# A hybrid mixer layer on one Trainium2 core: the depthwise convolutions read a copy of their product in SBUF, and the ring of divided weight tiles has four places

## The chip, the cores and the metric

One core of a Trainium2 chip runs the whole layer in one program. The metric is the device time of one execution in microseconds; three runs of the kernel before gave a median of 1195.45 us (1193.54 to 1199.78).

## What is computed

512 tokens of width 1024, in float32. One normalised input feeds four mixers side by side, each 512 wide (RWKV-7, gated linear attention, mLSTM, SSD), whose outputs are projected, weighted by gates and added; an output product and a gated feed-forward part with a short convolution follow. The piece that the change touches is the causal depthwise convolution with four taps, followed by SiLU, ahead of the SSD (1024 channels) and of the mLSTM's queries and keys (512 channels):

```python
def causal_dwconv(x, w, b):
    k, c = w.shape
    y = lax.conv_general_dilated(x, w[:, None, :].astype(x.dtype), window_strides=(1,),
                                 padding=((k - 1, 0),), dimension_numbers=('NWC', 'WIO', 'NWC'),
                                 feature_group_count=c)
    return y + b

q, k = _split(jax.nn.silu(causal_dwconv(qk, conv_w, conv_b)), (MLSTM_DQK, MLSTM_DQK))
x, bm, cm = _split(jax.nn.silu(causal_dwconv(xbc, conv_w, conv_b)), ...)
```

## The kernel before

**Products.** A float32 weight tile of 128x512 is loaded by SyncE's queue into `raw`, ScalarE casts it to `hi` (L225), and VectorE, in some places GpSimd, subtracts to get the rest, `lo` (L226). `split_h` does this. The pairs of hi and lo come from `w_tiles` (L217), a ring with three places for each. A product is three matmuls per 128 rows of the depth, hi by hi, hi by lo and lo by hi (`mm3`, L235 to L237). With 1024 inputs a tile of 128 output channels by 512 tokens takes 24 of them and fills one PSUM bank of `psd`, which has three. `fm` makes such a tile with channels as partitions; `tm` (L330 to L332, 256 columns) makes products with tokens as partitions, two banks at a time, each bank for two blocks of 128 tokens and half of the outputs; every weight pair is used by both banks.

**Convolution.** `conv4` is called for each `fm` tile: eight for the SSD (`ssd_x`, sx0 to sx7) and four for the mLSTM (`mlstm_proj`, mq0 to mq3). ScalarE writes `y` from the bank with the last tap's weight and the bias (L904), VectorE adds the three shifted taps, reading the bank each time (L907), ScalarE takes tanh (L909), and VectorE the last product (L910). The bank is free after the third L907.

**Order.** Nothing is issued in the order of the source alone: `TileContext(schedule_with_timeline_sim=True)` (L1331) orders the instructions of all engines ahead of the run, from priorities and its own estimate of durations. At run time each engine takes its queue strictly in that order and waits for semaphores. The program's stages overlap. In time: norm, RWKV projections, first RWKV half (`rwkv_half(0)`: an inverse by 31 rounds of L600 and L602 on VectorE, 129 to 172 us, then a loop over chunks, then a group norm that ends in the matmuls of L728 at 315 us), gated linear attention (`gla`, whose U recurrence is L832, whose masks are L845 and whose products with the masks are L854) and `ssd_x` between them, the SSD (`ssd`, L995), a projection for its z gate (`ssd_z`, `tm("sz", ...)`), the second RWKV half with its own inverse (488 to 528 us), the mLSTM, the output product, and the feed-forward part from 837 us to the end.

**The SSD's chain.** For each of four blocks of 128 tokens a broadcast (`sab`, two buffers, L1019) is loaded through DRAM, GpSimd and VectorE subtract from it (L1041, four instructions each), ScalarE takes exp (L1042), GpSimd masks it (L1043), VectorE multiplies (L1052), and TensorE uses it (L1056), which frees the buffer. L1031 transposes x, L1033 copies it, L1038 and L1039 scale it, L1062 and L1068 are the state's products, L1063, L1064, L1073 and L1074 what is done with them. The z gate's banks are read by ScalarE (L1084) and VectorE (L1085).

**The feed-forward part's first two products** (`fm_halves` at L1239) need four pairs at a time; three come from the ring, the fourth is a pair of its own, `wx`, in a pool `hw`.

Of the kernel before, what the change touches and what calls it, by code (L numbers as in the profile page):

```python
# [16 lines left out]
P = 128  # L17
T = 512
# [142 lines left out]
def kernel(ctx: ExitStack, tc: tile.TileContext, A, out):  # L161
    nc = tc.nc
    V, S, G, PE = nc.vector, nc.scalar, nc.gpsimd, nc.tensor
# [23 lines left out]
    wp = ctx.enter_context(tc.tile_pool(name="wp", bufs=1))  # L187
# [7 lines left out]
    def pd():  # L195
        return dense[0].tile([P, T], F32, tag="d", name="psd")
# [17 lines left out]
    def col(name, i=0, lo=0, hi=P):  # L214
        return pf[lo:hi, PF_AT[name] + i:PF_AT[name] + i + 1]

    def w_tiles():  # L217
        return (wp.tile([P, 512], F32R, tag="hi", name="hi", bufs=3), wp.tile([P, 512], F32R, tag="lo", name="lo", bufs=3))

    def split_h(src, h, tiles=None, eng=V):  # L220
        raw = wp.tile([P, 512], F32, tag="raw", name="raw", bufs=NRAW)
# [9 lines left out]
    def split_w(src, tiles=(None, None), eng=V):  # L231
        return [split_h(src, h, tiles[h], G if (pl[0] >> h) & 1 else eng) for h in range(2)]

    def mm3(ps, lh, ll, rh, rl, first, last):
        PE.matmul(ps, lh, rh, start=first, stop=False)  # L235
        PE.matmul(ps, lh, rl, start=False, stop=False)  # L236
        PE.matmul(ps, ll, rh, start=False, stop=last)  # L237
# [36 lines left out]
    def fm_halves(jobs, eng=V):  # L274
        ws = [split_w(src, tiles, eng) for src, tiles in jobs]
        pss = [pd() for _ in jobs]
        for h in range(2):
            ts = slice(256 * h, 256 * h + 256)
            for w, ps in zip(ws, pss):
                for k in range(KD):  # L280
                    hi, lo = w[k // 4]
                    ks = slice((k % 4) * P, (k % 4 + 1) * P)
                    mm3(ps[:, ts], hi[:, ks], lo[:, ks], uh[:, k, ts], ul[:, k, ts], k == 0, k == KD - 1)
        return pss
# [53 lines left out]
    def t2(pool=None):  # L338
        pl, n = pool or wpool
        return pl.tile([P, T], F32, tag="w", name="w", bufs=n)  # L340
# [559 lines left out]
        return res  # L900

    def conv4(ps, w, b, n, i, pool=None):
        y = t2(pool)
        S.activation(y, ps, AF.Identity, scale=col(w, 3 * n + i), bias=col(b, i))  # L904
        for k in range(3):
            d = 3 - k
            V.scalar_tensor_tensor(y[:, d:T], ps[:, 0:T - d], col(w, k * n + i), y[:, d:T], op0=ALU.mult, op1=ALU.add)  # L907
        th = t2(pool)
        S.activation(th, y, AF.Tanh, scale=0.5)  # L909
        V.scalar_tensor_tensor(y, th, 1.0, y, op0=ALU.add, op1=ALU.mult)  # L910
        return y
# [80 lines left out]
    def ssd_x():  # L992
        return [conv4(fm(f"sx{i}"), "scw", "scb", 8, i, (wk, NW)) for i in range(8)]
# [215 lines left out]
    nc.sync.dma_start(gb2, A["gvec"][D:2 * D].partition_broadcast(P))  # L1209
    gb3 = hp.tile([P, D], F32, name="gb3")  # L1210
    nc.sync.dma_start(gb3, A["gvec"][2 * D:3 * D].partition_broadcast(P))
    hw_ctx = ExitStack()
    hw = hw_ctx.enter_context(tc.tile_pool(name="hw", bufs=1, side="right", reuse_waits="tile"))
    wx = [hw.tile([P, 512], F32R, name=n) for n in ("wxh", "wxl")]
    hx = ExitStack()
    np_ = hx.enter_context(tc.tile_pool(name="nq", bufs=1, side="right", reuse_waits="tile"))

# [5 lines left out]
    for b in range(NB):  # L1223
# [12 lines left out]
        norm_T(h2[:, b], gb2, b, np_, uh, ul, 1, [pr_, pm])  # L1236
    tap("h2", h2)
    hx.close()
    first = fm_halves([(A["up"][0], (None, None)), (A["up"][1], (None, (wx[0], wx[1])))])  # L1239
    hw_ctx.close()  # L1240
    wo_ctx.close()
    mo_ctx.close()
    ps_ctx.close()
# [42 lines left out]
    for n in range(2):  # L1286
# [3 lines left out]
        for k in range(NF):  # L1290
            late = n == 1 and k >= NF - KT
            tiles = tuple(fp.tile([P, 512], F32R, tag="y", name="wl", bufs=6) for _ in range(2)) if late else None
            w = split_h(A["dn"][n * (NF // 2) + k // 2], k % 2, tiles)
# [41 lines left out]
```

## Time and profile before

| | |
|---|---|
| median of three runs | 1195.45 us (1193.54 to 1199.78) |
| the profiled execution | 1195.54 us |
| its span, first to last instruction | 1193.7 us |
| TensorE, VectorE, ScalarE, GpSimd busy | 96%, 55%, 37%, 28% of the span |
| chain that ended last | 74% TensorE, 11% VectorE, 7% DMA, 4% issue |
| costliest groups | 912 matmuls each at L235, L236 and L237, 358 us a line; 280 subtracts of L226 on VectorE, 229 us |

An engine's row gives its busy time; the idle time in front of an instruction is shown with what ended it. A matmul of 512 columns shows about 0.39 us, but one starts every 0.227 us, since they overlap. PEclk is the granted TensorE clock as a share of full speed.

### The profile page before, as it was taken

The numbers are of one execution on the slowest core, as the hardware profiler recorded it, in microseconds if no ns is written. First come the engines' busy times: TensorE is split into PE (matmuls) and PEld (weight loads), VectorE is DVE, ScalarE is ACT, GpSimd is POOL, SyncE is SP. The second block draws the span as 40 slices with busy tenths as digits, with TensorE's granted clock in tenths as the row PEclk, the third lists the DMA queues.
The fourth block names the chain that finished last, engine by engine and source line by source line (L and its number), as shares of the span: only waits on it lengthen the run. The fifth ranks groups of instructions, "written<-read, shape, count | busy, mean of one in ns | idle before, by whom it ended". The sixth has DMA issues, their size and how long they took to land.

```text
span 1193.7 us, 17895 instructions
## 1 busy us (share of the span) xinstructions
PE 1143.7 (96%) x6881; PEld 928.9 (78%) x6881; DVE 651.6 (55%) x1090; ACT 444.4 (37%) x820; POOL 331.4 (28%) x287
## 2 busy tenths in 40 slices
PE   5999989999999999989999999999999999999997
PEld 4887868777788767778777777778788888888886
DVE  5258796453576365793235653554665666652323
ACT  4355234332333432232124343432444444442323
POOL 3104012230285543331114543620212222220100
PEclk9999989999998999999999999999999999999999
DMA  5222322322341322332224523561232223222322
GB/s 198 65 98 64 88 61 70 103 78 79 105 98 53 98 80 67 93 83 91 68 84 150 160 88 115 184 201 38 89 101 96 96 96 99 97 97 97 97 97 107
DMA packets 79886, 117.30 MB, mean 98 GB/s; under 512 B 22660, under 2 KB 27172, under 8 KB 79800
## 3 DMA queue, kind: packets, MB, share of 16 engines
q1 hardware_dynamic: 79224, 115.11, 30.6%
q8 instruction: 54, 0.88, 0.3%
q10 hardware_dynamic: 576, 1.05, 0.2%
q14 instruction: 32, 0.26, 0.1%
HBM read 107.93 MB, written 8.19 MB: 97 GB/s over the span
## 4 chain that ended last, share of the span: by engine, by line
PE 74%; DVE 11%; DMA 7%; issue 4%; ACT 2%; POOL 1%; SPq 1%; POOLq 0%; DVEq 0%; ACTq 0%
PE psd L235 17%; PE psd L236 16%; PE psd L237 16%; PE psd L1282 3%; PE psd L1283 3%; PE psd L1284 3%; DVE Mi L602 2%; DVE Mt L600 2%; DMA sab<-ad 2%; DVE lo L226 1%; PE psr L676 1%; PE psd L331 1%; PE psd L330 1%; DMA raw<-in_wo_dram 1%; PE psd L332 1%
## 5 line engine op out<-in xcount | busy, mean ns | idle before, releaser
L226 DVE TENSOR_TENSOR lo<-raw,hi 128x512 fp32r<-128x512 f32 x280 | 229.0, 819 | 312.0 <-ACT hi L225 300.6
L225 ACT CAST hi<-raw 128x512 fp32r<-128x512 f32 x322 | 199.6, 620 | 485.7 <-PE psd L236 300.9
L235 PE MATMUL psd<-uh,hi 128*128 128x512 f32 (+1 forms) x912 | 359.9, 395 | 11.5 <-DVE w L907 4.8
L237 PE MATMUL psd<-uh,lo 128*128 128x512 f32 (+1 forms) x912 | 357.6, 393 | 4.5 <-DVE lo L226 4.1
L236 PE MATMUL psd<-ul,hi 128*128 128x512 f32 (+1 forms) x912 | 356.2, 391 | 0.2 <-DVE ul L252 0.2
L235 PEld LDWEIGHTS psd<-uh,hi 128*128 128x128 f32 x912 | 172.2, 189 | 53.0 <-ACT hi L225 6.2
L237 PEld LDWEIGHTS psd<-uh,lo 128*128 128x128 f32 x912 | 172.2, 189 | 44.8 <-DVE lo L226 5.6
L236 PEld LDWEIGHTS psd<-ul,hi 128*128 128x128 f32 x912 | 172.3, 189 | 36.8 <-issue 2.6
L226 POOL TENSOR_TENSOR lo<-raw,hi 128x512 fp32r<-128x512 f32 x42 | 56.9, 1356 | 194.2 <-ACT hi L225 157.5
L1271 POOL TENSOR_TENSOR y<-y 128x512 f32<-128x512 f32 x22 | 28.3, 1288 | 174.0 <-DVE y L1265 160.1
L1265 DVE SCALAR_TENSOR_TENSOR y<-psd,pf,y 128x510 f32<-128x510 f32 x88 | 65.9, 750 | 2.7
L1284 PE MATMUL psd<-hi,al 128*128 128x512 f32 x164 | 63.8, 389 | 0.0
L1283 PE MATMUL psd<-lo,ah 128*128 128x512 f32 x164 | 63.8, 389 | 0.0
L331 PE MATMUL psd<-lo,uh 128*128 128x256 f32 x192 | 57.1, 298 | 1.0 <-DVE lo L226 1.0
L1282 PE MATMUL psd<-hi,ah 128*128 128x512 f32 x164 | 57.3, 389 | 0.0
L332 PE MATMUL psd<-hi,ul 128*128 128x256 f32 x192 | 56.3, 294 | 0.0
L330 PE MATMUL psd<-hi,uh 128*128 128x256 f32 x192 | 55.8, 292 | 0.0
L331 PEld LDWEIGHTS psd<-lo,uh 128*128 128x128 f32 x192 | 37.8, 197 | 5.2 <-issue 3.3
L332 PEld LDWEIGHTS psd<-hi,ul 128*128 128x128 f32 x192 | 37.9, 197 | 1.3 <-issue 1.0
L330 PEld LDWEIGHTS psd<-hi,uh 128*128 128x128 f32 x192 | 37.7, 197 | 1.6 <-issue 1.2
L1284 PEld LDWEIGHTS psd<-hi,al 128*128 128x128 f32 x164 | 30.8, 188 | 6.5
L1282 PEld LDWEIGHTS psd<-hi,ah 128*128 128x128 f32 x164 | 30.8, 188 | 6.4
(418 smaller groups left out, 1696.5 us busy)
## 6 DMA issues: line engine op xcount, KB each, us to landing
raw<-in_wfm_dram SPq DMA_DIRECT2D x140, 256.0 KB, 2.6
raw<-in_up_dram SPq DMA_DIRECT2D x88, 256.0 KB, 2.5
raw<-in_dn_dram SPq DMA_DIRECT2D x44, 256.0 KB, 2.5
raw<-in_bp_dram SPq DMA_DIRECT2D x32, 256.0 KB, 2.7
raw<-in_wtm_dram SPq DMA_DIRECT2D x24, 256.0 KB, 2.6
raw<-in_wo_dram SPq DMA_DIRECT2D x16, 256.0 KB, 3.0
gd<-th SPq DMA_DIRECT2D x15, 256.0 KB, 2.1
th<-gd SPq DMA_DIRECT2D x15, 256.0 KB, 2.9
```

The lines of the kernel that those rows point to most:

```text
L225: S.copy(hi, raw)
L226: eng.tensor_tensor(lo, raw, hi.bitcast(F32), op=ALU.subtract)
L235: PE.matmul(ps, lh, rh, start=first, stop=False)
L236: PE.matmul(ps, lh, rl, start=False, stop=False)
L237: PE.matmul(ps, ll, rh, start=False, stop=last)
L330: PE.matmul(o, uh[:, k, bs], hi[:, cs], start=first, stop=False)
L331: PE.matmul(o, uh[:, k, bs], lo[:, cs], start=False, stop=False)
L332: PE.matmul(o, ul[:, k, bs], hi[:, cs], start=False, stop=last)
L1265: V.scalar_tensor_tensor(y[:, d:T], ps[:, 0:T - d], col("fcw", k * 44 + n), y[:, d:T], op0=ALU.mult, op1=ALU.add)
L1282: PE.matmul(ps, ah[:, k, bs], hi, start=(k == 0), stop=False)
L1283: PE.matmul(ps, ah[:, k, bs], lo, start=False, stop=False)
L1284: PE.matmul(ps, al[:, k, bs], hi, start=False, stop=(k == NF - 1))
```

## The change

`conv4` takes its second tile `th` at the start, and ScalarE copies the bank into it (L904 of the new kernel). The activation (L905) and VectorE's three taps (L908) read that copy, and tanh later overwrites it. The ring of weight tiles has four places each for hi and lo. The pool `hw` with the pair `wx` is gone, and the first two products of the feed-forward part take all four pairs from the ring. From L910 on the lines of both kernels agree up to L1211; behind that the new ones are three or four lower.

```diff
--- before.py
+++ after.py
@@ -215,7 +215,7 @@
         return pf[lo:hi, PF_AT[name] + i:PF_AT[name] + i + 1]
 
     def w_tiles():
-        return (wp.tile([P, 512], F32R, tag="hi", name="hi", bufs=3), wp.tile([P, 512], F32R, tag="lo", name="lo", bufs=3))
+        return (wp.tile([P, 512], F32R, tag="hi", name="hi", bufs=4), wp.tile([P, 512], F32R, tag="lo", name="lo", bufs=4))
 
     def split_h(src, h, tiles=None, eng=V):
         raw = wp.tile([P, 512], F32, tag="raw", name="raw", bufs=NRAW)
@@ -900,12 +900,12 @@
         return res
 
     def conv4(ps, w, b, n, i, pool=None):
-        y = t2(pool)
-        S.activation(y, ps, AF.Identity, scale=col(w, 3 * n + i), bias=col(b, i))
+        y, th = t2(pool), t2(pool)
+        S.copy(th, ps)
+        S.activation(y, th, AF.Identity, scale=col(w, 3 * n + i), bias=col(b, i))
         for k in range(3):
             d = 3 - k
-            V.scalar_tensor_tensor(y[:, d:T], ps[:, 0:T - d], col(w, k * n + i), y[:, d:T], op0=ALU.mult, op1=ALU.add)
-        th = t2(pool)
+            V.scalar_tensor_tensor(y[:, d:T], th[:, 0:T - d], col(w, k * n + i), y[:, d:T], op0=ALU.mult, op1=ALU.add)
         S.activation(th, y, AF.Tanh, scale=0.5)
         V.scalar_tensor_tensor(y, th, 1.0, y, op0=ALU.add, op1=ALU.mult)
         return y
@@ -1209,9 +1209,6 @@
     nc.sync.dma_start(gb2, A["gvec"][D:2 * D].partition_broadcast(P))
     gb3 = hp.tile([P, D], F32, name="gb3")
     nc.sync.dma_start(gb3, A["gvec"][2 * D:3 * D].partition_broadcast(P))
-    hw_ctx = ExitStack()
-    hw = hw_ctx.enter_context(tc.tile_pool(name="hw", bufs=1, side="right", reuse_waits="tile"))
-    wx = [hw.tile([P, 512], F32R, name=n) for n in ("wxh", "wxl")]
     hx = ExitStack()
     np_ = hx.enter_context(tc.tile_pool(name="nq", bufs=1, side="right", reuse_waits="tile"))
 
@@ -1236,8 +1233,7 @@
         norm_T(h2[:, b], gb2, b, np_, uh, ul, 1, [pr_, pm])
     tap("h2", h2)
     hx.close()
-    first = fm_halves([(A["up"][0], (None, None)), (A["up"][1], (None, (wx[0], wx[1])))])
-    hw_ctx.close()
+    first = fm_halves([(A["up"][0], (None, None)), (A["up"][1], (None, None))])
     wo_ctx.close()
     mo_ctx.close()
     ps_ctx.close()
```

The scheduler makes a new order from this on all engines, far from the convolutions too. Three places follow. A number behind a name tells buffers apart.

**The order at the first convs.** VectorE before: steps of the first inverse (Mt, Mi), the U recurrence of the gated linear attention (L832), the conv of sx0 (bank psd_2141), and the masks L845 that read psm_1835 and psm_1836.

```order
L602 TENSOR_TENSOR Mi_845<-Mi_845,Mt_846 64x10x22
L907 SCALAR_TENSOR_TENSOR w_2166<-psd_2141,pf_77,w_2166 128x509
L600 TENSOR_TENSOR Mt_846<-Ls_842,Mi_845 64x207
L907 SCALAR_TENSOR_TENSOR w_2166<-psd_2141,pf_77,w_2166 128x510
L602 TENSOR_TENSOR Mi_845<-Mi_845,Mt_846 64x9x23
L832 SCALAR_TENSOR_TENSOR w_1779<-w_1778,gdk_1690,w_1779 128x128
L907 SCALAR_TENSOR_TENSOR w_2166<-psd_2141,pf_77,w_2166 128x511
L845 TENSOR_TENSOR w_1869<-psm_1835,cst_76 128x512
L600 TENSOR_TENSOR Mt_846<-Ls_842,Mi_845 64x192
L832 SCALAR_TENSOR_TENSOR w_1780<-w_1779,gdk_1690,w_1780 128x128
L845 TENSOR_TENSOR w_1871<-psm_1836,cst_76 128x512
```

VectorE now, the last rows ahead of the masks; in front of these stand, from the inverse step 64x10x22 on, that step and three more of the inverse, another L908, the last conv step L910 and four more L832.

```order
L602 TENSOR_TENSOR Mi_845<-Mi_845,Mt_846 64x8x24
L832 SCALAR_TENSOR_TENSOR w_1779<-w_1778,gdk_1690,w_1779 128x128
L600 TENSOR_TENSOR Mt_846<-Ls_842,Mi_845 64x175
L832 SCALAR_TENSOR_TENSOR w_1780<-w_1779,gdk_1690,w_1780 128x128
L602 TENSOR_TENSOR Mi_845<-Mi_845,Mt_846 64x7x25
L832 SCALAR_TENSOR_TENSOR w_1777<-w_1780,gdk_1690,w_1777 128x128
L600 TENSOR_TENSOR Mt_846<-Ls_842,Mi_845 64x156
L832 SCALAR_TENSOR_TENSOR w_1778<-w_1777,gdk_1690,w_1778 128x128
L602 TENSOR_TENSOR Mi_845<-Mi_845,Mt_846 64x6x26
L832 SCALAR_TENSOR_TENSOR w_1779<-w_1778,gdk_1690,w_1779 128x128
L845 TENSOR_TENSOR w_1869<-psm_1835,cst_76 128x512
L845 TENSOR_TENSOR w_1871<-psm_1836,cst_76 128x512
```

The masks have moved behind the conv, behind the run of L832 and down in the inverse from the end of its 23rd to the end of its 26th round.

TensorE now, where the second conv's product (sx1, psd_2187) ends and the third's (sx2, psd_2233) begins; L854 multiplies by the first mask, w_1869.

```order
L841 MATMUL psm_1835<-w_1684,w_1685 32x32
L841 MATMUL psm_1836<-w_1684,w_1685 32x32
L236 MATMUL psd_2187<-ul_85,hi_2183 128x512
L237 MATMUL psd_2187<-uh_84,lo_2184 128x512
L854 MATMUL psm_1873<-w_1869,w_1423 128x4x32
L854 MATMUL psm_1873<-w_1869,w_1424 128x4x32
L235 MATMUL psd_2233<-uh_84,hi_2223 128x512
L236 MATMUL psd_2233<-ul_85,hi_2223 128x512
```

Before, L854 stood in the middle of sx1's matmuls; now it follows sx1 and stands ahead of sx2.

**The order in the SSD.** TensorE before, where block 0's L1056 is issued: the z gate's matmuls (psd_3463) stand on both sides of it.

```order
L331 MATMUL psd_3463<-lo_3467,uh_84 128x256
L332 MATMUL psd_3463<-hi_3466,ul_85 128x256
L330 MATMUL psd_3463<-hi_3466,uh_84 128x256
L331 MATMUL psd_3463<-lo_3467,uh_84 128x256
L1056 MATMUL psm_2779<-w_2755,sab_2738 128x64 x8
L1068 MATMUL psm_2790<-w_2756,sbt_2771 128x256 x2
L1049 MATMUL psr_2827<-cst_76,w_2346 128x128
L1049 MATMUL psr_2827<-cst_76,w_2391 128x128
L332 MATMUL psd_3463<-hi_3466,ul_85 128x256
L330 MATMUL psd_3463<-hi_3466,uh_84 128x256
```

TensorE now, the end of the stretch from the last matmul of bank psd_3600 to the first of psd_3601.

```order
L1048 MATMUL psr_2897<-w_2442,w_2350 128x128
L1048 MATMUL psr_2897<-w_2488,w_2396 128x128
L1049 MATMUL psm_2898<-cst_76,w_2350 128x128
L1049 MATMUL psm_2898<-cst_76,w_2396 128x128
L1062 MATMUL psr_2918<-w_2863,w_2442 128x256
L1062 MATMUL psr_2918<-w_2863,w_2488 128x256
L1068 MATMUL psr_2923<-w_2884,sbt_2899 128x256 x2
L1031 MATMUL psr_2939<-cst_76,w_2166 128x128
L1031 MATMUL psr_2939<-cst_76,w_2212 128x128
L1031 MATMUL psr_2939<-cst_76,w_2258 128x128
L1031 MATMUL psr_2939<-cst_76,w_2304 128x128
L330 MATMUL psd_3601<-hi_3604,uh_84 128x256
```

What stood there as L235 to L237 and L330 to L332 has moved ahead of L728: of the dense work only the 48 matmuls of psd_3600 are left between L728 and psd_3601.

VectorE now, the rows that free the bank psd_3470, which psd_3601 takes; its last reader is the second L1085 with that name.

```order
L1025 TENSOR_TENSOR sf_2931<-sab_2929,stk_2744 128x8
L1050 COPY sbt_2899<-psm_2898 128x256
L1038 TENSOR_TENSOR w_2883<-w_2881,sf_2868 128x512
L1041 TENSOR_SCALAR sab_2929<-sab_2929,stk_2744 128x128 x4
L1027 SCALAR_TENSOR_TENSOR sf_2931<-sf_2931,stk_2744 128x8
L1074 TENSOR_TENSOR w_2926<-w_2926,psr_2923 128x512
L1033 COPY w_2944<-psr_2939 128x512
L1038 TENSOR_TENSOR w_2946<-w_2944,sf_2931 128x512
L1085 SCALAR_TENSOR_TENSOR w_3466<-w_3466,psd_3470 128x256
L1085 SCALAR_TENSOR_TENSOR w_3466<-w_3466,psd_3600 128x256
L1095 TENSOR_TENSOR w_2761<-w_2761,w_3466 128x512
L1085 SCALAR_TENSOR_TENSOR w_3467<-w_3467,psd_3470 128x256
```

The reader of the bank stands behind L1041 of block 3 (sab_2929); before, the first L1085 followed L1038 of block 3 as well, but with dense work of other banks in TensorE's queue beside it.

**The order in the second inverse.** VectorE before, steps of the inverse and one lo tile, of a projection's weights.

```order
L600 TENSOR_TENSOR Mt_4275<-Ls_4271,Mi_4274 64x231
L602 TENSOR_TENSOR Mi_4274<-Mi_4274,Mt_4275 64x21x11
L600 TENSOR_TENSOR Mt_4275<-Ls_4271,Mi_4274 64x240
L602 TENSOR_TENSOR Mi_4274<-Mi_4274,Mt_4275 64x20x12
L600 TENSOR_TENSOR Mt_4275<-Ls_4271,Mi_4274 64x247
L602 TENSOR_TENSOR Mi_4274<-Mi_4274,Mt_4275 64x19x13
L600 TENSOR_TENSOR Mt_4275<-Ls_4271,Mi_4274 64x252
L226 TENSOR_TENSOR lo_5206<-raw_5203,hi_5205 128x512
L602 TENSOR_TENSOR Mi_4274<-Mi_4274,Mt_4275 64x18x14
```

VectorE now, the same lo tile, which is called lo_5214 here.

```order
L600 TENSOR_TENSOR Mt_4283<-Ls_4279,Mi_4282 64x207
L602 TENSOR_TENSOR Mi_4282<-Mi_4282,Mt_4283 64x23x9
L600 TENSOR_TENSOR Mt_4283<-Ls_4279,Mi_4282 64x220
L602 TENSOR_TENSOR Mi_4282<-Mi_4282,Mt_4283 64x22x10
L226 TENSOR_TENSOR lo_5214<-raw_5211,hi_5213 128x512
L600 TENSOR_TENSOR Mt_4283<-Ls_4279,Mi_4282 64x231
```

It stood behind the round 64x252 and now stands ahead of 64x231.

## Rows read from the trace of the kernel before

**Rows 1.** Cores of the kernel before: span and mean granted clock.
```profile
core 0: 1193.7 us, clock 0.984
```

**Rows 2.** Page, part 1: busy time, share of the span, instructions.
```profile
PE 1143.7 (96%) x6881; PEld 928.9 (78%) x6881; DVE 651.6 (55%) x1090; ACT 444.4 (37%) x820; POOL 331.4 (28%) x287
```

**Rows 3.** Waits of TensorE: line, releaser, us in total, times, longest.
```profile
PE psd L235 <- DVE w L907: 4.8, 1, 4.8
PE psd L237 <- DVE lo L226: 4.1, 4, 2.5
PE psd L235 <- ACT hi L225: 3.3, 4, 1.8
```

**Rows 4.** Windows: us, busy (x) of PE, PEld, DVE, ACT, POOL; PEclk, DMA, GB/s.
```profile
150.00:165.00 15.00, 10.16 (x128) 7.76 (x127) 14.76 (x30) 5.07 (x9) 3.87 (x3) 0.77 0.15 54
315.00:375.00 60.00, 55.68 (x352) 49.39 (x350) 40.42 (x82) 16.57 (x38) 41.84 (x34) 0.94 0.33 88
837.00:1180.00 343.00, 342.02 (x1509) 283.26 (x1510) 174.52 (x221) 135.83 (x221) 62.73 (x48) 1.00 0.29 95
```

**Rows 5.** The conv steps of VectorE: duration ns min/median/max, first and last start.
```profile
L907 DVE SCALAR_TENSOR_TENSOR w<-psd,pf,w x36: 728/748/751, 155.8 to 544.4; 128x509 f32<-128x509 f32 x12, 128x510 f32<-128x510 f32 x12, 128x511 f32<-128x511 f32 x12
...
L910 DVE SCALAR_TENSOR_TENSOR w<-w x12: 657/693/1727, 161.4 to 545.9; 128x512 f32<-128x512 f32 x12
```

**Rows 6.** A copy of a PSUM tile by ScalarE at another line.
```profile
L829 ACT COPY w<-psm x8: 585/588/594, 146.1 to 187.2; 128x512 f32<-128x512 f32 x8
```

**Rows 7.** Timeline of TensorE at two stalls: start us, us, [idle before <-releaser].
```profile
158.72 0.80 PE L235 MATMUL psd<-uh,hi 128*128 128x512 f32 x1 [4.78 <-DVE w L907]
...
516.03 0.50 PE L237 MATMUL psd<-uh,lo 128*128 128x512 f32 x1 [2.46 <-DVE lo L226]
```

**Rows 8.** Timeline of VectorE at the first conv.
```profile
153.51 0.38 DVE L600 TENSOR_TENSOR Mt<-Ls,Mi 64x220 f32<-64x220 f32 x1
...
154.42 1.44 DVE L602 TENSOR_TENSOR Mi<-Mi,Mt 64x220 f32<-64x220 f32 x1
...
157.67 0.34 DVE L832 SCALAR_TENSOR_TENSOR w<-w,gdk 128x128 f32<-128x128 f32 x1
```

**Rows 9.** Page, part 5: the hi casts of the weights.
```profile
L225 ACT CAST hi<-raw 128x512 fp32r<-128x512 f32 x322 | 199.6, 620 | 485.7 <-PE psd L236 300.9
```

**Rows 10.** Timeline of TensorE at both ends of the SSD stage.
```profile
315.14 1.04 PE L728 MATMUL psr<-cst,Yt 128*128 128x128 f32 x8
...
374.95 0.36 PE L330 MATMUL psd<-hi,uh 128*128 128x256 f32 x1
```

**Rows 11.** Timeline of VectorE in the SSD stage.
```profile
325.87 0.17 DVE L1025 TENSOR_TENSOR sf<-sab,stk 128x8 f32<-128x8 f32 x1 [2.32 <-DMA sab<-ad]
...
340.57 1.29 DVE L1052 SCALAR_TENSOR_TENSOR sab<-psr,sab 128x512 f32<-128x512 f32 x2 [1.09 <-POOL sab L1043]
...
343.43 1.49 DVE L1038 TENSOR_TENSOR w<-w,sf 128x512 f32<-128x512 f32 x1
```

**Rows 12.** Timeline of GpSimd in the SSD stage.
```profile
326.21 4.00 POOL L1041 TENSOR_SCALAR sab<-sab,stk 128x128 f32<-128x128 f32 x4 [5.88 <-ACT sf L1023]
...
330.18 1.04 POOL L1039 TENSOR_TENSOR w<-w,sf 128x512 f32<-128x512 f32 x1
...
335.34 5.20 POOL L1043 TENSOR_TENSOR sab<-sab,cst 128x1024 f32<-128x1024 f32 x2
...
352.35 1.29 POOL L1064 TENSOR_TENSOR w<-w 128x512 f32<-128x512 f32 x1
```

**Rows 13.** Tile sab, 316 to 375: ns min/median/max; landing us.
```profile
L1041 POOL TENSOR_SCALAR sab<-sab,stk x16: 707/773/1666, 326.2 to 360.7; 128x128 f32<-128x128 f32 x16
...
L1042 ACT ACTIVATE sab<-sab x4: 1058/1061/1062, 330.2 to 361.4; 128x1024 f32<-128x1024 f32 x4
...
DMA to landing us min/median/max: 5.5/6.3/7.8
```

**Rows 14.** Timeline of GpSimd there.
```profile
154.02 1.60 POOL L226 TENSOR_TENSOR lo<-raw,hi 128x512 fp32r<-128x512 f32 x1 [3.42 <-PE psm L841]
```

## The prediction

> **What bounds the kernel now.** I read from the outside in. One core, 1193.7 us of span at a mean granted clock of 0.984 [rows 1]. The profiled execution took 1195.54 us, the median of three runs is 1195.45 (1193.54 to 1199.78), so what is worked out on its trace may be added to the median as it stands. TensorE is busy for 1143.7 us, 96% [rows 2]. No change can gain more than what TensorE stands still or runs at half clock: 50 us of idle, and 1.6% of the span, 19 us, of lost clock.
>
> Where TensorE stands still is in the list of its waits [rows 3]: 4.8 us once for the last read of a bank by the conv (L907), 4.1 us for four lo tiles, 3.3 us for four hi tiles. At these three the change can gain. The last part of the program, 837 to 1180, has 342.0 us of busy TensorE in 343, 1509 matmuls, 0.2266 us each at full clock [rows 4]: nothing is to be had there.
>
> **The conv.** Twelve tiles go through `conv4`. Each has three VectorE steps of 748 ns that read PSUM and a last one with two SBUF inputs, 693 ns [rows 5]. Now ScalarE copies the bank first; such a copy takes 588 ns at L829 [rows 6]. 12 x 0.59 = 7 us go to ScalarE; where the first convs run, it is busy 5.1 us in 15 [rows 4], so I cost that at nothing. If that cover is gone, which needs a conv's result to be waited for at once, it is 0.59 us a place. The three steps have two SBUF inputs now. At the last step's median each saves 0.055 us, 2 us over 36, off the path; its mean is 788 and its longest 1727 ns, so they can also lose. On the path I take 0.
>
> The bank is free after one copy, not after four reads that stand among other work. Does the stall at 153 go? TensorE stood 4.78 us until 158.72 [rows 7], and in 15 us around it was busy for 10.2 at a granted clock of 0.77 [rows 4]. In the new order sx1 starts without that wait. But the L845 mask, which stood right behind the third conv step, now stands behind another conv step, a last conv step, nine L832 and nine steps of the inverse, and TensorE's L854, which needs it, stands ahead of sx2 (the order at the first convs). From the inverse step at 154.42, at 0.34 for an L832, 0.38 for an inverse step [rows 8], 0.7 for each conv step and the mask: 9 x 0.34 + 9 x 0.38 + 3 x 0.7 = 8.6 us, and one to three meetings with GpSimd of 1 us each (below): done at 164 to 166. TensorE, with the rest of sx0, then sx1 and L841 before it, gets there at about 159.5: sx1's 24 matmuls are 5.4 us, and L841 ended 5 us before 158.72. **The stall moves from L907 to L854**, 4 to 7 us. I take +1 (-5 if it is covered, +4 if the inverse, which then ends later, makes the RWKV loop wait).
>
> **The fourth tile.** Hi casts waited 300.9 us in all for a matmul to release a tile [rows 9]: the ring of three was full most of the time, a cast starts when a tile comes back, and its subtract then waits its turn in VectorE's queue. With four, the second inverse (488 to 528 us) has its lo subtracts four to six rounds earlier in that queue (the order in the second inverse). The longest such stall was there, 2.46 us until 516.03 [rows 7]. Of the 7.4 us of these waits [rows 3] I take 7 away, and 1.3 us for matmuls that ran slowly behind them: -8.3. The ends are 0, if each subtract is only late elsewhere, and -11. The two tiles `wx` are replaced by tiles of the ring in a stretch where TensorE doesn't wait: 0.
>
> **What the new order costs.** Tiles that come early let dense work run early. That dense work was the cover of the SSD's chain. I count from the first L728, which ends the first RWKV half, to the first matmul of the last z bank (bank 3593 then, 3601 now):
>
> - Before: 70 matmuls of 512 columns at 0.2266 and 132 of 256 at half of that, 30.8 us of dense work, in the 59.8 us from 315.14 to 374.95 [rows 10]. TensorE idled 60 - 55.7 = 4.3 us in that stretch and lost 6% of clock, 3.6 us [rows 4]; the SSD's own matmuls and transposes took the rest, 59.8 - 30.8 - 4.3 - 3.6 = 21.1.
> - Now: 48 of 256 columns, 5.4 us. No more can run: the two z banks of the first half are parked until L1084 and L1085 have read them, the third is being filled, and all four ring tiles stay with the second z half. In the order of the SSD there is no dense row between the last of bank 3600 and 3601.
>
> How long is the chain then? L728 to the first sab block landed, 315.14 to 325.87: 10.7 us [rows 10, 11]. Then GpSimd sets the pace: two blocks' L1041 and L1043 from 326.21 to 340.54, +25.4 [rows 12]. Block 1 then had L1052 to L1038, 340.57 to 344.92 [rows 11], with a subtract among them that is gone now; L1056 frees its buffer at about +30. The transfer of block 3 into it lands 6.3 us later [rows 13], +36.4. GpSimd is by then the later one again: four L1041 of block 2 (4.0, up to about +36), L1064, L1039 and another product (1.3, 1.0, 1.0), four L1041 of block 3 (4.0) [rows 12]: done at +43 to +44. ScalarE's L1084 of the second row block stands behind L1042 of block 3 (1.06 [rows 13]), VectorE's L1085 behind that, 0.4 each: the bank is free at about **+45.7**. Dense work 5.4 and SSD steps 17.6 (16 L1056 and six others, 3.5 of the 21.1, come later) leave 23 us of idle where 4.3 stood.
>
> Like with like: the new kernel needs 45.7 + 3.5 = 49.2 us for what the old one does in 59.8 - (30.8 - 5.4) = 34.4. **+14.8 us.** Bounds: +7 if GpSimd's sixteen L1041, which meet fewer subtracts now, run near their shortest (0.71 and not 1.0 [rows 13], 4 us) and blocks 2 and 3 overlap better; +20 if they run at their longest in part. Behind a long idle matmuls ran at the lower clock level (0.77 on the mean around 153 [rows 4]); before's own loss is in the 34.4 already, so +1 for that, 0 to 3.
>
> **The sum:** conv 0, stall at 153 +1, fourth tile -8.3, SSD +14.8, clock +1 = +8.5: 1195.5 + 8.5 = 1204 us. A change under 0.5%, 6 us, can hardly be told from none here.
>
> **The port.** An inverse step of 0.38 us at 153.51 takes 1.44 at 154.42 [rows 8], while GpSimd runs L226 from 154.02 for 1.60 us [rows 14]; the conv's last step, with two SBUF inputs, went up to 1727 ns, the three that read PSUM never over 751 [rows 5]. The Trainium skill, page "SBUF — State Buffer", section "Who interferes with whom", says that a VectorE instruction with two SBUF inputs contends with a GpSimd instruction that reads SBUF, and one with at most one such input doesn't. By that rule the change exposes 36 steps that were safe; the trace of before agrees for the last step alone, since no row of it has the new three.
>
> **The rivals.**
> 1. *Faster.* The SSD loses only some 2 us, since GpSimd, with fewer neighbours, is done with the blocks 12 us sooner; with -8.3 for the fourth tile and the stall at 153 gone, -5: 1195.5 - 11 = 1184. For it: three waits that have names vanish, and L1041's shortest is 0.71. Against: the order shows no dense row in the gap. It decides where the z bank is free by +33.
> 2. *No difference.* SSD +8, fourth tile -8.3, stall 0 to +1: 1195 to 1197. For it: the bounds of both terms meet. That the copy doesn't do what it is said to do, because the bank is seldom the wait (once in twelve, 4.8 us), ends here too.
> 3. *The port on top.* GpSimd is busy 3.9 us in 15 around the first convs [rows 4], a quarter; of 36 steps nine meet it, +1.0 each; those that stand in the inverse's way are of the first three tiles, 2.5 us, so 1206.5. It decides if the mean of the three steps is over 1.0 us.
>
> **How the numbers follow.** Forecast, with its own range 1200 to 1210: 0.41; the port on top: 0.09; together slower by over 0.5% (above 1201.5): 0.5, the forecast's lower edge being made up for by the upper bounds. No difference 0.29. Faster 0.21. The range goes from 1185, which takes in half of rival 1, to 1212, where the SSD's upper bound meets most of the gains: 8 in 10.
>
> **What would show it.** Right: between L728 and the last z bank some 23 us of idle TensorE, in few long waits for L1052, for blocks 2 and 3 and for L1085; a wait at L854 of 4 to 7 us in place of the one at L907; the waits for hi and lo of 7.4 us down to about 1; conv steps of 0.69 us alone and 1.4 or more beside GpSimd. Wrong: under 10 us of idle there; no wait at L854; new waits in the mLSTM or after 837, where the order hardly moves.

## The result, and the profile after

The changed kernel took 1231.79 us (1228.82 to 1234.95, four runs) against 1194.49 (1192.93 to 1199.78) for the kernel before on the same chip: a ratio of 1.0305 [1.0259, 1.0350], 37 us slower. The forecast was 1204, with a range of 1185 to 1212. The direction was right; the size was off by a factor of more than four, 37 us against 8.5.

The profiled execution took 1228.82 us, so it is the fastest of the four; its span is 33.3 us longer than that of before [rows 1]. First the busy times of the page, which answer to [rows 2]:

```profile
PE 1152.8 (94%) x6881; PEld 938.3 (76%) x6881; DVE 658.4 (54%) x1090; ACT 453.0 (37%) x832; POOL 333.9 (27%) x287
```

TensorE issues the same 6881 matmuls, 9.1 us longer in sum, and stands idle for 74 us where it stood for 50. The list of its waits says where (line, releaser, us in total, times, longest; the counterpart of [rows 3]). Its first row, the norm at the program's start, is left out here: 11.8 us, and 12.6 before.

```profile
PE psm L1056 <- DVE sab L1052: 8.9, 1, 8.9
PE psd L235 <- DVE w L424: 5.7, 1, 5.7
PE psr L629 <- DMA MN<-mnd: 5.4, 1, 5.4
PE psd L330 <- DVE w L1085: 4.6, 1, 4.6
PE psm L854 <- DVE w L845: 4.5, 1, 4.5
PE psd L235 <- DVE w L1085: 3.3, 1, 3.3
...
PE psd L237 <- DVE lo L226: 0.7, 1, 0.7
```

Two of these waits stood in the list of before too, but were shorter:

```profile
PE psm L1056 <- DVE sab L1052: 3.2, 1, 3.2
PE psr L629 <- DMA MN<-mnd: 0.6, 1, 0.6
```

The lo waits of 4.1 us are down to 0.7, the one for L907 is gone. In their place stand two in the SSD that the forecast names (L1052 and the first L1085), the one at L854 that it names, and three that it doesn't: L424, the second L1085, and L629 of the second inverse. TensorE's timeline puts them in order:

```profile
166.16 1.22 PE L854 MATMUL psm<-w 128*128 128x128 f32 x4 [4.52 <-DVE w L845]
...
343.28 0.93 PE L728 MATMUL psr<-cst,Yt 128*128 128x128 f32 x7
...
365.42 1.33 PE L1056 MATMUL psm<-w,sab 128*128 128x64 f32 x5 [8.88 <-DVE sab L1052]
...
390.54 0.58 PE L330 MATMUL psd<-hi,uh 128*128 128x256 f32 x1 [4.60 <-DVE w L1085]
...
429.33 0.50 PE L235 MATMUL psd<-uh,hi 128*128 128x512 f32 x1 [3.29 <-DVE w L1085]
...
438.69 1.88 PE L460 MATMUL psm<-w,cst 128*4 128x512 f32 x4 [0.27 <-ACT w L1106]
...
446.27 0.80 PE L235 MATMUL psd<-uh,hi 128*128 128x512 f32 x1 [5.70 <-DVE w L424]
...
455.84 0.55 PE L494 MATMUL psr<-cst,w 128*128 128x128 f32 x3 [1.93 <-DVE w L481]
...
571.73 0.28 PE L629 MATMUL psr<-MN,zm 32*32 32x32 f32 x2 [5.42 <-DMA MN<-mnd]
```

L728 stood at 315.14 before [rows 10] and stands at 343.28 now, 28 us later. That is not a loss yet: the order has put dense work ahead of it. I call **dense** the matmuls of the weight products and count them in the order, at 0.2266 us for 512 columns and half of that for 256, as in the prediction. Ahead of L728 stand 207.1 us of them before and 233.9 now, 26.8 more. A stage's **extra** is how much longer it takes, plus the dense work that it no longer holds (minus what it holds on top).

Behind L728 come three stages: the SSD up to the last L1056; its output (L1085, the norm, the transposes of L1104); and what I call the norm chain, the keys' norm of the second RWKV half. That one goes from the last L460 on TensorE through DRAM to `nn` (L466 on VectorE, then GpSimd's power) and through DRAM again to the tile that VectorE's L524 reads. In VectorE's queue a first L424 stands behind L466, a second L424 and L481 behind L524, and TensorE's transposes L494 need L481; I count to the first L494.

The windows of both kernels for the SSD, its output and the norm chain (us, busy of PE, PEld, DVE, ACT, POOL, PEclk, DMA, GB/s), before:

```profile
315.14:374.87 59.73, 55.41 (x349) 49.21 (x348) 40.28 (x82) 16.56 (x37) 41.84 (x34) 0.94 0.33 89
374.87:393.59 18.72, 18.72 (x114) 16.69 (x114) 12.65 (x20) 9.20 (x21) 6.18 (x5) 1.00 0.28 85
402.95:419.06 16.11, 16.11 (x70) 12.83 (x69) 5.56 (x9) 5.47 (x10) 8.55 (x7) 1.00 0.39 128
```

and after, the SSD also in two parts, up to the first matmul of the last z bank and from there:

```profile
343.28:404.98 61.70, 42.83 (x244) 38.33 (x242) 36.46 (x76) 15.19 (x36) 42.42 (x36) 0.78 0.18 52
343.28:390.54 47.26, 28.39 (x154) 24.52 (x152) 26.99 (x64) 11.32 (x28) 33.27 (x30) 0.77 0.20 56
390.54:404.98 14.44, 14.44 (x90) 13.81 (x90) 9.48 (x13) 3.87 (x9) 9.15 (x7) 0.80 0.11 37
404.98:436.52 31.54, 28.25 (x123) 23.20 (x123) 10.70 (x18) 10.24 (x19) 7.47 (x6) 0.95 0.27 89
439.98:455.84 15.86, 8.23 (x26) 5.79 (x24) 2.96 (x6) 5.30 (x10) 8.76 (x7) 0.78 0.15 46
```

| us | before: elapsed, dense in it | after: elapsed, dense in it | extra |
|---|---|---|---|
| up to the first L728 | 315.1, 207.1 | 343.3, 233.9 | +1.3 |
| SSD | 59.7, 30.8 | 61.7, 12.9 | +19.9 |
| its output, to the first L1104 | 18.7, 18.1 | 31.5, 25.2 | +5.7 |
| to the last L460 | 9.4, 5.9 | 3.5, 0 | 0 |
| norm chain | 16.1, 15.4 | 15.9, 5.2 | +10.0 |

At the first L494 of the second half both kernels have done the same dense work (277.4 and 277.1 us), and the new one is 36.8 us late (455.84 against 419.06). From there to the end it takes 3.5 us less, which makes the 33.3 of the two spans. **Nearly the whole loss, 35.6 of the 36.8 us, lies in these three stages. Two of them, the SSD and the norm chain, are chains of small steps that last about as long as before, with 17.9 and 10.2 us less dense work to run beside.** In the SSD 14.6 of the 19.9 us are idle (18.87 against 4.32); the rest stands beside a clock of 0.78 where it was 0.94. The output is a different case: it holds 7.1 us more dense work than before, but TensorE waits 3.3 us for the bank that the second L1085 frees, and runs at a clock of 0.95 where it was 1.00.

### The profile page after: what moved, and what is told of

It reads as the page before. It is cut to its first block, busy times and chain, and to the rows that moved or that the text cites. A ratio compares the mean times of both kernels' runs of the same rounds, so it can differ in the third digit from the quotient of the medians.

```text
span 1227.0 us, 17898 instructions
## 1 busy us (share of the span) xinstructions
PE 1152.8 (94%) x6881; PEld 938.3 (76%) x6881; DVE 658.4 (54%) x1090; ACT 453.0 (37%) x832; POOL 333.9 (27%) x287
## 5 line engine op out<-in xcount | busy, mean ns | idle before, releaser
L235 PE MATMUL psd<-uh,hi 128*128 128x512 f32 (+1 forms) x920 | 360.1, 393 | 14.7 <-DVE w L424 5.7
L237 PE MATMUL psd<-uh,lo 128*128 128x512 f32 (+1 forms) x920 | 359.7, 392 | 0.7 <-DVE lo L226 0.7
L235 PEld LDWEIGHTS psd<-uh,hi 128*128 128x128 f32 x920 | 174.5, 190 | 54.5 <-DVE w L424 6.6
L237 PEld LDWEIGHTS psd<-uh,lo 128*128 128x128 f32 x920 | 174.5, 190 | 38.7 <-issue 1.8
L1261 DVE SCALAR_TENSOR_TENSOR y<-psd,pf,y 128x510 f32<-128x510 f32 x88 | 65.6, 747 | 2.5
L1278 PE MATMUL psd<-hi,ah 128*128 128x512 f32 x164 | 63.8, 389 | 0.0
L330 PE MATMUL psd<-hi,uh 128*128 128x256 f32 x192 | 59.3, 310 | 4.6 <-DVE w L1085 4.6
L332 PE MATMUL psd<-hi,ul 128*128 128x256 f32 x192 | 57.9, 302 | 0.0
L330 PEld LDWEIGHTS psd<-hi,uh 128*128 128x128 f32 x192 | 39.8, 207 | 8.7 <-DVE w L1085 4.8
L332 PEld LDWEIGHTS psd<-hi,ul 128*128 128x128 f32 x192 | 39.8, 207 | 2.1 <-issue 1.7
L908 DVE SCALAR_TENSOR_TENSOR w<-w,pf 128x509 f32<-128x509 f32 (+2 forms) x36 | 32.5, 904 | 6.4 <-ACT w L905 5.9
L1279 PEld LDWEIGHTS psd<-lo,ah 128*128 128x128 f32 x164 | 30.8, 188 | 6.4
```

The source lines that it names most:

```text
L330: PE.matmul(o, uh[:, k, bs], hi[:, cs], start=first, stop=False)
L332: PE.matmul(o, ul[:, k, bs], hi[:, cs], start=False, stop=last)
L1261: V.scalar_tensor_tensor(y[:, d:T], ps[:, 0:T - d], col("fcw", k * 44 + n), y[:, d:T], op0=ALU.mult, op1=ALU.add)
L1278: PE.matmul(ps, ah[:, k, bs], hi, start=(k == 0), stop=False)
L1279: PE.matmul(ps, ah[:, k, bs], lo, start=False, stop=False)
```

## The experiments

**Two halves of the change.** First the copy alone, with the ring of three and `wx` kept:

```diff
-        y = t2(pool)
-        S.activation(y, ps, AF.Identity, scale=col(w, 3 * n + i), bias=col(b, i))
+        y, th = t2(pool), t2(pool)
+        S.copy(th, ps)
+        S.activation(y, th, AF.Identity, scale=col(w, 3 * n + i), bias=col(b, i))
...
-            V.scalar_tensor_tensor(y[:, d:T], ps[:, 0:T - d], col(w, k * n + i), y[:, d:T], op0=ALU.mult, op1=ALU.add)
-        th = t2(pool)
+            V.scalar_tensor_tensor(y[:, d:T], th[:, 0:T - d], col(w, k * n + i), y[:, d:T], op0=ALU.mult, op1=ALU.add)
```

> The convolutions read the SBUF copy; the ring keeps three places and wx stays. Theory A (the loss comes from the order that the fourth tile brings, which takes the cover from the SSD's chain): in the order 207 us of dense work stand before the first L728 and 30.8 us inside the SSD, as in the kernel before, so 1190 to 1199 us, 59 to 63 us from L728 to the SSD's last L1056, and the bank wait at L907 gone. Rival B (the copy lengthens each conv's chain and exposes its steps to GpSimd, and that is the loss): 1210 us or more.

Measured: 1197.0 us (1195.6 to 1200.67, ten runs) against 1195.67, ratio 1.0018 [1.0005, 1.0032]: within theory A's range.

Then the ring of four without `wx`, with the old convolution:

```diff
-        return (wp.tile([P, 512], F32R, tag="hi", name="hi", bufs=3), wp.tile([P, 512], F32R, tag="lo", name="lo", bufs=3))
+        return (wp.tile([P, 512], F32R, tag="hi", name="hi", bufs=4), wp.tile([P, 512], F32R, tag="lo", name="lo", bufs=4))
...
-    first = fm_halves([(A["up"][0], (None, None)), (A["up"][1], (None, (wx[0], wx[1])))])
+    first = fm_halves([(A["up"][0], (None, None)), (A["up"][1], (None, None))])
```

> Four places in the ring and no wx; the convolutions read PSUM as before. Theory A: the order puts 228 us of dense work before the first L728 and leaves 11 us of it until the last z bank, so nearly the whole loss: 1220 to 1236 us. Rival B (the copy is the loss): 1190 to 1200 us. In between, 1203 to 1217, both parts are needed.

Measured: 1230.81 us (1227.36 to 1237.99), ratio 1.0295 [1.0257, 1.0333], again within theory A's range. The ring (with `wx` gone) makes nearly the whole loss, the copy next to none. With the old convolution 228.2 us of dense work stand ahead of L728, and the windows of its SSD and norm chain read:

```profile
340.93:403.09 62.16, 46.60 (x293) 41.55 (x292) 37.98 (x80) 16.88 (x39) 43.01 (x36) 0.86 0.26 69
438.10:454.00 15.90, 8.32 (x26) 5.87 (x24) 2.96 (x6) 5.29 (x10) 8.74 (x7) 0.79 0.14 47
```

The SSD holds 18.7 us of dense work here, which makes its extra +14.5; the norm chain's is +10.0 again.

The copy's kernel shows the moved stall by itself, and TensorE's SSD much as before (timeline, then window):

```profile
165.79 1.44 PE L854 MATMUL psm<-w 128*128 128x128 f32 x5 [4.80 <-DVE w L845]
...
321.92:382.27 60.35, 54.65 (x347) 48.68 (x346) 40.56 (x82) 16.96 (x37) 40.69 (x34) 0.94 0.32 84
```

**The fourth place only where no chain is left.** The ring keeps three places until the second RWKV projection; from there every fourth request takes a place of its own:

```diff
+    ring = [3, 0]
     def w_tiles():
+        ring[1] += 1
+        e = "4" if ring[0] == 4 and ring[1] % 4 == 0 else ""
+        return tuple(wp.tile([P, 512], F32R, tag=n + e, name=n, bufs=1 if e else 3) for n in ("hi", "lo"))
...
     pl[0] = Q["L_p1"]
+    ring[0] = 4
```

> The copy as in the new kernel; the fourth place of the ring is handed out only from the second RWKV half on. Theory A: 207 us of dense work before L728 as before, the waits for hi and lo behind 420 us gone: 1186 to 1195 us. Rival C (four places hurt wherever they are, since tiles that come early take VectorE's and ScalarE's time from chains): 1203 us or more.

Measured: 1205.11 us (1203.61 to 1205.52), ratio 1.0070 [1.0055, 1.0085]: of 37 us some 28 are gone. Theory A's range of 1186 to 1195 was missed all the same, and the time lies in rival C's. In the two chains rival C isn't seen: again 207.1 us of dense work stand ahead of L728 and 30.8 in the SSD, whose extra is +2.3; the norm chain's is +0.2. This kernel has no `wx` either, so the missing pair alone doesn't uncover the chains.

```profile
320.38:382.40 62.02, 56.82 (x347) 50.43 (x346) 40.97 (x83) 17.49 (x38) 40.62 (x34) 0.92 0.31 81
410.82:426.92 16.10, 16.01 (x69) 12.50 (x67) 5.10 (x9) 5.73 (x10) 8.64 (x7) 1.00 0.40 132
```

It is still 8 us behind the copy alone. At the first L494 of the second half the two are level (426.92 and 426.90), so that loss lies behind it. Its list of waits (lines stand four to five higher here) has the second inverse's one, and one at the feed-forward part's start, where `wx` is missing; the copy alone shows neither, and the kernel before 1.5 us of the second (L1265 there):

```profile
PE psr L633 <- DMA MN<-mnd: 3.9, 2, 3.6
PE psd L239 <- DVE y L1266: 3.5, 1, 3.5
```

Whether rival C holds there, behind the two chains, stays open.

**Is the norm chain paced by TensorE's wait at L424, or by itself?** The list of waits blames L424. VectorE's timeline shows why L424 was late in the new kernel: it stands behind L466 in VectorE's queue, and that waited 10.4 us for `nn`. Before, VectorE stood only 0.3 us in front of L466 (first two rows, then the new kernel):

```profile
407.13 0.18 DVE L466 TENSOR_SCALAR nn<-nn 128x16 f32<-128x16 f32 x1 [0.33 <-DMA nn<-nq]
415.21 0.75 DVE L524 SCALAR_TENSOR_TENSOR w<-w,pf 128x512 f32<-128x512 f32 x1 [2.29 <-DMA w<-nd]
...
445.38 0.28 DVE L466 TENSOR_SCALAR nn<-nn 128x16 f32<-128x16 f32 x1 [10.41 <-DMA nn<-nq]
445.47 0.74 DVE L424 SCALAR_TENSOR_TENSOR w<-psd,pf,w 128x511 f32<-128x511 f32 x1
453.71 0.75 DVE L524 SCALAR_TENSOR_TENSOR w<-w,pf 128x512 f32<-128x512 f32 x1 [7.50 <-DMA w<-nd]
```

So L466 went to GpSimd, and L424 no longer stands behind it:

```diff
-        V.tensor_scalar(nn, nn, scalar1=1e-24, scalar2=None, op0=ALU.max)
+        G.tensor_scalar(nn, nn, scalar1=1e-24, scalar2=None, op0=ALU.max)
```

> The new kernel with one step, L466 (128x16), on GpSimd's queue and not on VectorE's. In the new kernel it stood 10.4 us in VectorE's queue for its DMA, with L424 behind it, which frees a bank that TensorE waited 5.7 us for. Theory D (this wait in a queue is a loss of its own, 5 to 6 us, of the 37): 1225 to 1228 us. Rival E (the chain behind it, L460 to L524, ends last anyway): within 1.5 us of the new kernel's 1231.8.

Measured: 1236.27 us (1235.22 to 1238.26), ratio 1.0335 [1.0320, 1.0350]: not faster than the new kernel. That rules out theory D; it is also 3 us above what rival E allowed. The timelines of VectorE and TensorE:

```profile
458.42 0.75 DVE L524 SCALAR_TENSOR_TENSOR w<-w,pf 128x512 f32<-128x512 f32 x1 [10.90 <-DMA w<-nd]
...
447.57 0.79 PE L235 MATMUL psd<-uh,hi 128*128 128x512 f32 x1 [3.16 <-DVE w L424]
...
460.54 0.90 PE L494 MATMUL psr<-cst,w 128*128 128x128 f32 x3 [6.01 <-DVE w L481]
```

The wait at L424 fell from 5.7 to 3.2 us, and the one at L494 rose from 1.9 to 6.0, since L481 now stands behind an L524 that waits 10.9 us for the chain's second transfer, where it waited 7.5. The chain's own length doesn't fall: from the last L460 on TensorE to the first L524 on VectorE it is 14.6 us here, 13.7 in the new kernel, 12.3 in the one before, and between those in every other kernel of this study. (In this one GpSimd's memset L610 stands between L466 and the power, 0.95 us.) Whoever stands first behind a step of it in the queue shows the wait. What is left is dense work beside it, or another order of VectorE's queue, with L481 ahead of L524; the latter wasn't tried.

**GpSimd's pace in the SSD.** The forecast has GpSimd set it. One setting of the kernel gives the four subtracts of L1041 wholly to VectorE (its 0.29 us against GpSimd's 0.71). In the new kernel, and as a control in the kernel before:

```diff
-    E_xd=0, E_ah=1, E_dd=0,
+    E_xd=0, E_ah=0, E_dd=0,
```

> The new kernel, with all 32 steps of L1041 on VectorE (16 of them were on GpSimd, 2.8 to 3.5 us per block). Theory A: in the new kernel nothing covers the SSD's chain, and GpSimd sets its pace, so each of the blocks 0, 1 and the pair 2 and 3 is ready some 2 to 3 us sooner and TensorE gets that time: 5 to 10 us off 1231.8, 1222 to 1227. Rival F (the transfers of sab and VectorE's own queue set the pace): within 2.5 us of 1231.8.

> The same edit on the kernel before, as a control. Theory A: there 30.8 us of dense work cover that chain, TensorE waits 3.2 us once for L1052 in it, so at most 3 us are gained: 1191.5 to 1196. If as much is gained here as in the new kernel, the cover is not what sets the two apart.

Measured: 1226.49 us (1224.49 to 1228.31), ratio 1.0268 [1.0236, 1.0299], in the new kernel; 1198.2 (1193.93 to 1202.53), ratio 1.0030 [1.0010, 1.0051], in the one before. The first lies in theory A's range, 5 us under the new kernel, but the two intervals of the ratio overlap. The control missed its range: it was to gain at most 3 us and lost 3 to 4. Its order has moved too, and its norm chain holds 11.6 us of dense work in place of 15.4. In the profile of the new kernel with it, SSD and norm chain read

```profile
351.10:406.96 55.86, 38.34 (x192) 33.58 (x190) 38.81 (x88) 11.92 (x30) 26.65 (x18) 0.68 0.18 48
436.02:453.11 17.09, 16.92 (x74) 13.26 (x72) 5.10 (x9) 5.80 (x10) 8.89 (x7) 1.00 0.38 124
```

From L728 to the first L494 it takes 102.0 us (351.10 to 453.11) where the new kernel takes 112.6: 10.5 gained. Of that 9.7 are the norm chain's, since this order leaves it 16.1 us of dense work and its extra is then +0.3. The SSD is 5.8 us shorter, but holds 7.5 us less dense work too, so its extra is not smaller (+21.5). That GpSimd's pace is what the SSD costs is therefore not shown: the edit moved the order as well. In this profile L728 comes 7.8 us later than in the new kernel's, though the same 233.9 us of dense work stand ahead of it (on this, the last section).

**Can the cover be put back by the order?** Three settings were meant to move the z gate's projection or the gates of the first half, and with them dense work, past L728.

```diff
-    P_br1=60,
+    P_br1=0,
```

> The new kernel with the priority of branch 1's gates at 0: in the order they go behind the SSD, the z gate stays in front of it, and 206.7 us of dense work stand before L728 as in the kernel before, but only 5.4 us inside the SSD. Theory A (what counts is the cover inside the SSD's chain, not how much runs before it): the SSD's 20 us are lost as in the new kernel, while the norm chain behind it (L460 to L494) has its cover back, so 1215 to 1226. Rival G (the loss comes from packing 26 us more into the first RWKV loop): 1200 us or less.

Measured: 1232.62 us (1231.97 to 1233.16), ratio 1.0319 [1.0291, 1.0347]. The 206.7 us of dense work that the expectation puts ahead of L728 are the next kernel's, not this one's: here the order is the new kernel's but for little, 12.8 us in the SSD and 5.2 in the norm chain, and so is the time. It shows only that this priority doesn't move the cover.

With the z gate's projection written between the two parts of the gates:

```diff
-    ZP=0,
+    ZP=2,
```

> The new kernel with the z gate written between the first four and the last four gates of branch 1, so that the scheduler puts it earlier. In the order 207 us of dense work stand before the first L728, as in the kernel before, but only 14 us from there to the SSD's last L1056 (30.8 before, 12.9 in the new kernel), while the norm chain (L460 to L494) has 17 us again (15.4 before, 5.2 in the new). Theory A (the cover inside each chain counts): some 20 us lost in the SSD as in the new kernel, and the 9.5 us of the norm chain not lost: 1215 to 1224. Rival G (the loss comes from packing more into the first RWKV loop): 1203 or less. Rival H (something else of the four-place ring): 1229 to 1234.

and ahead of both:

```diff
-    ZP=0,
+    ZP=1,
```

> The new kernel with the z gate written before all gates of branch 1. In the order 174 us of dense work stand before L728, 33 less than in the kernel before, 14 us in the SSD, and 60.5 us between the second norm's transposes (L1104) and L460, 17 in the norm chain. Theory A: the same loss in the SSD and none in the norm chain, so as the run before it, 1215 to 1224, within 4 us of it although 33 us of work stand elsewhere. Rival G: 1203 or less, and lower than the run before it.

Measured: 1231.38 us (1225.89 to 1232.41), ratio 1.0281 [1.0238, 1.0324], and 1233.94 (1231.08 to 1239.24), ratio 1.0323 [1.0282, 1.0363]. Neither is a gain, though both have the norm chain covered, as expected: theory A's 1215 to 1224 was missed twice, and the first lies in the range of rival H. Rival G is ruled out. The windows of the first (the group norm ahead of L728, the SSD, the norm chain) and its timeline say why:

```profile
322.42:332.67 10.25, 1.25 (x16) 1.01 (x12) 5.35 (x7) 1.32 (x2) 3.48 (x3) 0.65 0.00 0
332.67:400.24 67.57, 46.04 (x232) 39.65 (x233) 38.62 (x82) 18.28 (x43) 38.20 (x34) 0.72 0.18 51
443.59:461.27 17.68, 17.68 (x77) 14.08 (x76) 8.62 (x11) 8.17 (x15) 13.48 (x10) 1.00 0.32 106
...
332.67 1.73 PE L728 MATMUL psr<-cst,Yt 128*128 128x128 f32 x7 [9.00 <-DVE Yt L723]
...
353.21 1.97 PE L1056 MATMUL psm<-w,sab 128*128 128x64 f32 x8 [12.54 <-DVE sab L1052]
```

The norm chain has 17.0 us of dense work and loses nothing. But what covers it came from the group norm of the first half, a fourth chain of some 10 us, which held 11.3 us of dense work before, 12.9 in the new kernel, and holds 0.8 here: TensorE waits 9.0 us at L728 for L723 (10.0 in the second kernel), and that stage's extra is +8.6 (+9.5). This fourth chain was found after the result; theory A as put on record didn't have it. The SSD's extra is +24.6 and +24.3; why that stage lasts 67 us here, 6 more than in the new kernel, was not traced. The second kernel has only 174.0 us of dense work ahead of L728, 33 less than the kernel before, and is no faster: so the loss is not that the first half's loop is packed with too much, it is which chain goes without.

The extras of all kernels, and how much longer they take behind the first L494 (us against the kernel before; the short stage up to the last L460, at most 0.4 us, is left out):

| | dense ahead of L728 | up to L728 | SSD | output | norm chain | behind L494 | ratio |
|---|---|---|---|---|---|---|---|
| copy alone | 207.1 | +6.8 | +0.6 | +0.4 | 0 | -5.6 | 1.0018 |
| fourth place late | 207.1 | +5.2 | +2.3 | +0.4 | +0.2 | +1.4 | 1.0070 |
| ring of four alone | 228.2 | +4.7 | +14.5 | +5.9 | +10.0 | -3.1 | 1.0295 |
| the change | 233.9 | +1.3 | +19.9 | +5.7 | +10.0 | -3.5 | 1.0305 |
| L466 on GpSimd | 233.9 | +4.3 | +20.8 | +5.7 | +10.8 | -1.1 | 1.0335 |
| L1041 on VectorE | 233.9 | +9.2 | +21.5 | +3.0 | +0.3 | -1.3 | 1.0268 |
| the same, kernel before | 207.1 | +2.2 | -0.4 | +1.1 | +2.4 | -3.5 | 1.0030 |
| gates' priority 0 | 234.1 | +3.2 | +20.6 | +5.9 | +10.0 | -3.2 | 1.0319 |
| z between the gates | 206.7 | +17.9 | +24.6 | -0.4 | 0 | -5.3 | 1.0281 |
| z before the gates | 174.0 | +15.5 | +24.3 | -0.4 | 0 | +0.1 | 1.0323 |

The column up to L728 holds the group norm in the last two rows, and in every row differences of the clock from execution to execution (last section). The copy's small total is the difference of two larger numbers, 7.8 us late at the first L494 and 5.6 gained behind it; what makes either was not traced.

A ring of four with `wx` kept wasn't tried. No kernel of the study beat the kernel before.

## Why the prediction was wrong in size

**The step that failed is the end of the account.** "What the new order costs" was counted "from the first L728 ... to the first matmul of the last z bank", with 5.4 us of dense work left there where 30.8 had been. Within those bounds the sum nearly holds: the bank came free at +45.7 by the forecast and L330 starts at 390.54, +47.3, which in the prediction's own sum is 47.3 + 3.5 - 34.4 = +16.4 for its +14.8. Its inside was less exact: TensorE idles 18.9 us there, not 23, and is busy for 28.4, not 23. But 26.8 us of dense work had left the time behind L728, and dense work that is missing is missing for each chain that comes later, not for the next one alone. The SSD's output (+5.7) and the norm chain (+10.0) were not looked at. The order of TensorE, which I had, shows the latter: nothing dense stands between the first L1104 and the last L460, and 5.2 us where 15.4 stood behind it.

The terms, forecast and measured: up to L728 +1 and +1.3, SSD with its clock +15.8 and +19.9, output and norm chain 0 and +15.7, all that lies behind them -8.3 and -3.5. Of the 25 us between +8.5 and +33.3, the two stages that were left out are 15.7, the tile that gave back too little 4.8, the SSD 4.1.

The signs that were to tell right from wrong could not catch this: idle time in the SSD, the wait at L854 and the shorter waits for hi and lo came as said, and none of the signs of being wrong did. All of them look at the stretch that was costed.

**Clock, +1 (0 to 3).** The SSD's extra is 5.3 us beyond its idle time, at a clock of 0.78 where before had 0.94. The lower of the two levels was granted not only just behind the waits: from 390.54 to 404.98 TensorE never stands idle, and the mean clock is still 0.80.

**The fourth tile, -8.3 (0 to -11).** The waits for hi and lo went as forecast, 7.4 us down to under 1, and gave little back. Behind the first L494 the new kernel takes 3.5 us less, for everything, and the copy alone, with three places, takes 5.6 less; so not even the 3.5 can be put down to the tile. Counted from the first L494, TensorE arrives 3.8 us sooner at the second inverse's end and waits 5.4 us there for `MN`, where it waited 0.6: the inverse on VectorE sets that stage, not the lo tile. It takes 42.7 us now (523.3 to 565.9) and took 39.9 (487.7 to 527.6). The lower end of the term, "if each subtract is only late elsewhere", had the right form.

**The stall at 153, +1.** Right in its mechanism: the wait moved from L907 (4.78) to L854 (4.52 in the new kernel, 4.80 with the copy alone), within the 4 to 7 us forecast. That the kernel is just 1.3 us late at L728 is in part luck, since the clock alone moves that by several us between executions (last section).

**The conv, 0.** Right in the sum, since the copy alone costs some 2 us in all, and wrong in what a step saves. Groups of the new kernel by line (ns min/median/max), which answer to [rows 5]:

```profile
L908 DVE SCALAR_TENSOR_TENSOR w<-w,pf x36: 733/750/1776, 156.2 to 577.3; 128x509 f32<-128x509 f32 x12, 128x510 f32<-128x510 f32 x12, 128x511 f32<-128x511 f32 x12
...
L904 ACT COPY w<-psd x12: 576/581/602, 151.4 to 572.8; 128x512 f32<-128x512 f32 x12
...
L905 ACT ACTIVATE w<-w,pf x12: 815/818/830, 152.4 to 573.4; 128x512 f32<-128x512 f32 x12
```

The three steps take 750 ns from SBUF and took 748 from PSUM [rows 5]; no 0.055 us was saved.

**The wx pair, 0.** Small in the new kernel: the wait for y at the feed-forward part's first convolution is 2.1 us (L1261), and was 1.5. Where the rest is mended it is 3.5 us, with the fourth place late.

**The rivals.** *Faster* was to decide by a z bank free at +33; it was +47.3. *No difference* needed the fourth tile's -8.3, which didn't come. *The port on top* needed a mean of the three steps over 1.0 us; it was 0.90. The meetings themselves did happen: six of 36 took 1525 to 1776 ns, each beside an instruction of GpSimd, and the sum of the 36 is 32.5 us (36 x 0.748 = 26.9 before). Here are VectorE and GpSimd at one of them:

```profile
181.53 3.22 DVE L908 SCALAR_TENSOR_TENSOR w<-w,pf 128x509 f32<-128x509 f32 x3
...
182.62 1.58 POOL L226 TENSOR_TENSOR lo<-raw,hi 128x512 fp32r<-128x512 f32 x1 [8.31 <-ACT hi L225]
```

Before, five of the 36 steps ran beside such a subtract of GpSimd, and none took more than 751 ns [rows 5]. The Trainium skill, page "SBUF — State Buffer", section "Who interferes with whom", has a VectorE instruction with two SBUF inputs contend with a GpSimd instruction that reads SBUF, and one with at most one such input not; the trace agrees. Not each meeting costs: a step at 169.01 took 739 ns with GpSimd's L790 beside it throughout. The 5.6 us are VectorE's. The ring of four alone has none of them (its 36 steps sum to 26.7 us) and takes 1230.8 us against 1231.8, so at most a part of them shows in the time; the intervals are too wide to tell how much.

## What to carry to other kernels

In this kernel a deeper ring of weights let dense work run early, and with TensorE 96% busy that was no gain: the dense work was the cover of the latency chains (small steps that wait for each other) that come later, and each chain needs its own. Before such a change, list every chain behind the point where the work moves (its length, the dense work beside it in the old order and the new), down to where both orders have done the same dense work, and sum what is short in all of them. A wait named in the list is a place in a queue: if it goes and the chain behind it stays, the next in the queue shows it.

## What the runs showed of the hardware that was not expected

Reading a float32 tile of 512 columns from SBUF in place of PSUM was no faster: VectorE's step 750 ns against 748, ScalarE's activation 818 against 772. This is ScalarE's line in the kernel before, to set beside L905 above:

```profile
L904 ACT ACTIVATE w<-psd,pf x12: 768/772/775, 151.6 to 540.8; 128x512 f32<-128x512 f32 x12
```

The granted clock differs between executions where the order doesn't. The new kernel and the one with L1041 on VectorE have the same order of TensorE in their first 1400 matmuls, but for one that comes three places later; yet these windows differ; the new kernel, then the other:

```profile
110.00:120.00 10.00, 10.00 (x96) 8.55 (x94) 6.14 (x10) 8.68 (x15) 2.44 (x2) 0.85 0.22 52
```
```profile
110.00:120.00 10.00, 10.00 (x56) 7.76 (x55) 4.43 (x7) 7.49 (x13) 0.68 (x1) 0.50 0.10 17
```

TensorE is busy throughout in both; at 0.50, the lower level of 1.2 GHz, it gets through 56 matmuls in place of 96. This is most of the 7.8 us by which L728 comes later in that profile. The new kernel's own four runs fall into 1228.8 and 1229.6, 1233.9 and 1235.0; that this is the same clock was not shown. What makes the clock rise in the one execution and not in the other stays open, and so do up to some 6 us of any single profile here: the stretch in which the dense work goes from 60 to 70 us took 31.5 us in the new kernel's profile, 37.6 in the other, and 28.8 in that of the kernel before.
